# A planner that books a change of first partition, with one padded operand split in two, one product chain made a stream of its own and one fetch moved later

## The chip, the core and the metric

The kernel runs on one core of one Trainium2 chip. The metric is device time in microseconds (us) of one execution on that core. Five engines work side by side, each through a queue of its own in program order: TensorE (PE: matmuls; PEld: its weight loads), VectorE (DVE), ScalarE (ACT), GpSimd (POOL) and SyncE (SP), which here only issues DMAs.

## What is computed

One decoder layer over 272 prompt rows (16 of them meta tokens) and 8 x 4 sample rows, 304 columns in all. Cut to what matters:

```python
xn = rms_norm(x, norm_mix);  z = xn @ w_in               # 2048 x 7456
z_a, z_b = z[..., :RWKV_COLS], z[..., RWKV_COLS:]
# RWKV-7 group, 16 heads of 64
S = S * w_t + sa * b_t + v_t * k_t;  o_t = S @ r_t        # per token, sa = S @ a_t
o = group_norm(o) * ln_w + ln_b
bonus = jnp.sum(rh * kh * r_k, axis=-1, keepdims=True) * vh
o_a = (o + bonus) * g
# retention group, 4 heads of 256, chunked
o_b = retention(z_b)
h = x + concat(o_a, o_b) @ w_out
h = h + (silu(rms_norm(h) @ w_gate) * (rms_norm(h) @ w_up)) @ w_down
y = rms_norm(h)
```

The outputs are y, the last projected rows and the new states.

## The kernel before, in words

**Main job list.** All weights go through one sequence of jobs (`sequence`, `main`): 59 column tiles of the input projection, 2 x 16 tiles of the output projection, then the FFN. A job runs k-steps; a k-step is three f32r matmuls into a PSUM bank `acc` (xh by wh, xl by wh, xh by wl, the operands split into a high and a low part), 304, 290 or 288 columns wide. Weights come by SP into `wr` (3 tiles of 1024 columns); ACT casts 512 columns at a time into `wh`, DVE forms the rest `wl`.

**Streams.** Everything else is a set of generators (`streams`), each of which issues a step and yields. Two heads together are a pair (`pair`, 8 of them). A pair prepares its operands, forms 64-token chunk scores against a zero-padded operand (`arp`, two heads side by side), inverts a triangular matrix (`inverse`: four small matmul groups, inv0 to inv3), computes the bonus (`bonus`), runs the state loop (`units`: for u = 0 to 4 three products, here called A, B and C of unit u), and normalises the output (`pair_out`). `by_token`, `sample` (the 8 x 4 sample rows, with their old state `s0`, 256 KB by DMA) and `ret` (the 4 retention heads) are streams too. Their matmuls are plain f32 into banks `mm`. In the state loop and in `inverse` the results go out of PSUM by halves: one instruction on partitions 0 to 63, one on 64 to 127 (`HALF`).

**What sets the order.** The program is built twice. In the draft, `Plan.book` prices each instruction and keeps a clock for each engine; `pick` lets a stream take its next step when its last step's results are ready by the plan's PE clock, and otherwise the main job goes on by one k-step. The picks are logged and the second build repeats them, so each engine's order is fixed when the kernel runs. Half-partition instructions are priced by `part`: DVE adds 80 ns, ACT adds 10 ns or takes 90 ns off when there is a per-partition scale. `Room` then gives each scratch tile a place in one arena by the draft's times (`place`, `pack`).

**The fetch of s0.** `lora_weights(p, 0)`, started when the pair's first input tile is out, issues the pair's low-rank weights and `s0` one behind the other on SP; `pair` waits for both.

Of the kernel before, what the change touches and what calls it, by code (L numbers as in the profile page):

```python
# [9 lines left out]
F32R = mybir.dt.float32r  # L10
# [5 lines left out]
P = 128  # L16
# [3 lines left out]
META = 16  # L20
NB = 8
# [57 lines left out]
WIDE = 4200  # L79
FREE, GAPS = 800.0, (2000.0, 1000.0, 500.0, 200.0, 0.0)  # L80

# [225 lines left out]
class Plan:  # L307
# [5 lines left out]
    def __init__(self, nc, rooms, draft, log, keep):  # L313
        self.keep = keep
        self.rooms, self.draft, self.log, self.count = rooms, draft, log, 0
        self.clock = dict(PE=0.0, DVE=0.0, ACT=0.0, POOL=0.0, SP=0.0)
        self.end = self.dma = 0.0
        self.uses, self.outside, self.banks = {}, (), set()
        self.mode, self.parts, self.empty, self.begun, self.idle = None, {}, 0.0, 0.0, 0.0
        self.taken = {"DVE": [], "POOL": []}  # L320
        self.streams, self.made = [], 0
# [27 lines left out]
    def book(self, eng, what, a, k):  # L349
# [20 lines left out]
        else:  # L370
            part = out.shape[0] < P
            each = sum(math.prod(x.shape[1:]) == 1 for x in ins) if n > 1 else 0
# [7 lines left out]
            else:  # L380
                dur, tail = (60 + 0.85 * n, 60) if what == "memset" else (125 + 0.8 * n, 65) if what == "tensor_copy" else (185 + 1.65 * n, 60)
            if part and eng == "DVE":
                dur += 80
            if part and eng == "ACT" and (each or n == 320):
                dur += 10 if ins[0].name not in self.banks else -90
            self.started = max(self.clock[eng], at)
            at = self.share(eng, what, ins, self.started, dur, each) + dur
# [36 lines left out]
    def array(self, what, out, w, x, ready):  # L424
# [15 lines left out]
        at = max(self.parts.get(part, self.empty), self.begun + 5)  # L440
        self.idle += max(0.0, ready - at)
        at = max(at, ready)
        self.begun = at
# [41 lines left out]
class Room:  # L485
# [20 lines left out]
    def place(self, limit):  # L506


        best = None
        for key in (lambda n, a, b, *_: (-n, a), lambda n, a, b, *_: (-n * (b - a), a), lambda n, a, *_: (a, -n),  # L510
                    lambda n, a, b, *_: (a - b, -n), lambda n, a, b, *_: (-n // 256, a - b)):
            for gap in GAPS:
                found = self.pack(key, limit, gap)
                if found is not None and (best is None or found[0] < best[0]):
                    best = found
        self.lack, self.size, self.places = best

    def pack(self, key, limit, gap):
        done, places, lack, end = [], [0] * len(self.spans), 0.0, 0
        used = [i for i, span in enumerate(self.spans) if span[1] is not None]  # L520
        for i in sorted(used, key=lambda i: key(*self.spans[i])):
            size, a, b, at, until = self.spans[i]
            size = -(-size // 8) * 8
            near = []
            for o, n, c, d, s, u in done:
                if a <= d and c <= b:
                    near.append((o, o + n, -1.0))
                else:
                    free = max(0.0, at - u if d < a else s - until)
                    if free < gap:  # L530
                        near.append((o, o + n, free))
            near.sort()
            best = None
            for o in sorted({0, *(e for _, e, _ in near)}):
                if o + size > limit:
                    break
                free = min((f for s, e, f in near if s < o + size and o < e), default=gap)
                if free > -1.0 and (best is None or free > best[0]):
# [3 lines left out]
            if best is None:  # L542
                return None
            lack += max(0.0, FREE - best[0])
# [21 lines left out]
class Step:  # L566
# [340 lines left out]
    def lora_weights(self, p, half, z):  # L907
# [3 lines left out]
        self.sp.dma_start(lw, self.I["lora"][p, :, 2 * half:2 * half + 2])  # L911
        if not half:
            z["s0"] = self.t([P, NB, 64], "s0")
            self.sp.dma_start(z["s0"], self.I["s0w"][p])
        yield
# [27 lines left out]
    def pair(self, p, z):  # L943
        cst, act, dve, pe, pool = self.cv, self.act, self.dve, self.pe, self.pool
        blk = cst("blk", P)
        while p >= PAIRS and ("mid", p - PAIRS) not in self.done:
            yield
        while not all(("lora", i) in self.done for i in range(3)) or len(z) < 5:
            yield
# [5 lines left out]
        pw = self.ps()  # L955
        k, r, v, s0, (wh, wl) = z["k"], z["r"], z["v"], z["s0"], z["lora", 0]
        xw, xa = self.xw
# [40 lines left out]
        dve.tensor_mul(bk[:, 1, :], kf, ee)  # L998
        dve.tensor_mul(ra[:, 1, META:], r[:, META:], dd[:, META:])
        yield  # L1000
        dve.tensor_mul(ta, ta, kk)
        dve.tensor_mul(ra[:, 0, :], kk, dp)
        arp = self.t([P, NU, 2, 2, 64], "arp")
        bku = self.t([P, NU, P], "bku")
# [4 lines left out]
        d4 = self.t([P, NB, 1], "d4")  # L1009
        pool.memset(arp[:, 0], 0.0)  # L1010
        for hi, h in enumerate(HALF):
            pool.memset(arp[h, 1:, :, 1 - hi], 0.0)
        pool.memset(bku[:, 0], 0.0)
        pool.memset(v0, 0.0)
        yield
        dve.tensor_mul(bk[:, 0, :], ta, ee)
        pool.memset(ax, 0.0)
        pool.memset(axd, 0.0)
# [9 lines left out]
        for hi, h in enumerate(HALF):  # L1028
            act.copy(arp[h, 0, 0, hi, :META], ra[h, 0, :META])
            act.copy(arp[h, 1:, :, hi], units(ra[h]))  # L1030

# [43 lines left out]
        for i, h in enumerate(HALF):  # L1075
            act.copy(sc[h, :, 0, i, :], arp[h, :, 0, i, :])
            pool.memset(sv[h, 0, i, :], 0.0)
# [13 lines left out]

    def bonus(self, r, kf, v, rkb):

# [6 lines left out]
        yield  # L1100
        bon = self.t([P, TO], "bon")
        self.dve.tensor_mul(bon[:, :SEQ], pq[:, :SEQ], v[:, META:NP])
        self.dve.tensor_mul(four(bon[:, SEQ:]), four(pq[:, SEQ:TO]), smp(v))
        return bon

# [106 lines left out]

    def units(self, p, sc, bkt, sv, sav, tt, arp, dl, o):

# [35 lines left out]
        for u in range(1, NU):  # L1250
            out = pt[:, (u - 1) * P:u * P]
            pe.matmul(out, flat(sv, u), arp[:, u, 1].rearrange("p h c -> p (h c)"), start=True, stop=False)
            pe.matmul(out, flat(sav, u), sc[:, u, 1].rearrange("p h c -> p (h c)"), start=False, stop=True)
# [516 lines left out]
def flat(a, u):  # L1770
    return a[:, u].rearrange("p h c -> p (h c)")
# [39 lines left out]
```

## Time and profile before

| | |
|---|---|
| median of 3 runs | 1567.49 us (1567.10 to 1567.64) |
| the profiled execution | 1568.03 us |
| its span, first to last instruction | 1566.0 us |
| instructions | 30584 |
| PE busy, PEld busy | 1545.0 us, 1509.6 us |
| DVE, ACT, POOL busy | 1097.1, 861.7, 27.9 us |
| granted TensorE clock, mean | 0.997 |

PE is the engine that hardly rests. A busy PE is not a PE at its peak: matmuls overlap and their ends are modelled. So a matmul's cost is read here from start to start in the timeline: what a matmul delays is the start of the next one. The mixing, with its streams, lies between about 60 and 640 us; after it only the main job list runs.

### The profile page before, as it was taken

To read this page: it belongs to the slowest core of one execution; us is meant where nothing else is said; L and a number is where in the kernel's file an instruction comes from. 1 tells how busy PE (TensorE), PEld (TensorE's weight loads), DVE (VectorE), ACT (ScalarE), POOL (GpSimd) and SP (SyncE) were. 2 spreads that over 40 slices of the span, in tenths; PEclk is the share of its full clock that TensorE was granted. 3 is DMA by queue.
4 is the path that set the end of the run, shared out by engine and by line. 5 is a ranking of instruction groups with operands and counts; after the bars stand their busy time and mean duration, and the time that the engine had idled before them with its cause. 6 is when DMAs were issued, how large, how long until landed. Compare 5 with 4: busy or idle time off the path is not lost.

```text
span 1566.0 us, 30584 instructions
## 1 busy us (share of the span) xinstructions
PE 1545.0 (99%) x11388; PEld 1509.6 (96%) x11388; DVE 1097.1 (70%) x2783; ACT 861.7 (55%) x2008; POOL 27.9 (2%) x145
## 2 busy tenths in 40 slices
PE   9999999999999999999999999999999999999997
PEld 8999999998989999999999999999999999999997
DVE  7899888987989776776555565555565656565657
ACT  6777878687777655555444444444444444444445
POOL 1000000000000000000000000000000000000000
PEclk9999999999999999999999999999999999999998
DMA  7543433434544536755555555555555555555553
GB/s 256 158 145 113 119 113 124 133 97 137 193 148 147 196 121 238 247 164 161 163 173 162 169 159 171 162 164 168 168 161 175 161 164 163 173 164 169 157 173 118
DMA packets 76995, 252.46 MB, mean 161 GB/s; under 512 B 9392, under 2 KB 14640, under 8 KB 76848
## 3 DMA queue, kind: packets, MB, share of 16 engines
q1 hardware_dynamic: 76848, 250.52, 51.0%
q8 instruction: 90, 1.47, 0.4%
q14 instruction: 57, 0.47, 0.1%
HBM read 236.21 MB, written 14.28 MB: 160 GB/s over the span
## 4 chain that ended last, share of the span: by engine, by line
PE 72%; DVE 3%; ACT 3%; issue 1%; DVEq 0%; ACTq 0%
PE acc L302 67%; PE mm L302 6%; DVE arena_dt.float L302 2%; ACT arena_dt.float L302 2%; DVE wl L302 1%; ACT wh L302 0%; ACT arena_dt.float32r L302 0%; DVE arena_dt.float32r L302 0%; DVEq L1807 0%; ACT shout L302 0%; ACTq L302 0%; DVEq L302 0%
## 5 line engine op out<-in xcount | busy, mean ns | idle before, releaser
L302 PE MATMUL acc<-xh,wh 128*128 128x288 f32 (+2 forms) x2592 | 795.6, 307 | 0.0
L302 PE MATMUL acc<-xh,wl 128*128 128x288 f32 (+2 forms) x2592 | 769.2, 297 | 0.0
L302 PE MATMUL acc<-xl,wh 128*128 128x288 f32 (+2 forms) x2592 | 767.4, 296 | 0.0
L302 ACT CAST wh<-wr 128x512 fp32r<-128x512 f32 x826 | 501.2, 617 | 347.5 <-PE acc L302 331.2
L302 DVE TENSOR_TENSOR wl<-wr,wh 128x512 fp32r<-128x512 f32 x826 | 561.3, 687 | 133.7 <-ACT wh L302 131.1
L302 PEld LDWEIGHTS acc<-xl,wh 128*128 128x128 f32 x2592 | 489.7, 189 | 4.2 <-issue 1.0
L302 PEld LDWEIGHTS acc<-xh,wh 128*128 128x128 f32 x2592 | 488.4, 188 | 4.7 <-issue 1.8
L302 PEld LDWEIGHTS acc<-xh,wl 128*128 128x128 f32 x2592 | 486.1, 188 | 0.4
L302 PE MATMUL acc<-arena_dt.float32r,wh 128*128 128x288 f32 x1408 | 282.4, 296 | 0.4 <-ACT arena_dt.float32r L302 0.3
L302 PEld LDWEIGHTS acc<-arena_dt.float32r,wh 128*128 128x128 f32 x1408 | 226.0, 188 | 0.8 <-ACT arena_dt.float32r L302 0.5
L302 PE MATMUL acc<-arena_dt.float32r,wl 128*128 128x288 f32 x704 | 208.0, 295 | 0.0
L302 DVE TENSOR_TENSOR arena_dt.float<-acc,arena_dt.float 128x288 f32<-128x288 f32 (+4 forms) x181 | 72.8, 421 | 166.9 <-PE acc L302 166.4
L302 DVE TENSOR_TENSOR arena_dt.float<-arena_dt.float 128x288 f32<-128x288 f32 (+23 forms) x697 | 179.7, 288 | 12.0 <-ACT arena_dt.float L302 5.2
L302 PE MATMUL mm<-arena_dt.float 128*128 128x128 f32 (+5 forms) x1072 | 170.3, 312 | 4.0 <-ACT arena_dt.float L302 2.6
L302 ACT ACTIVATE arena_dt.float<-arena_dt.float 128x288 f32<-128x288 f32 (+6 forms) x242 | 103.9, 436 | 118.9 <-DVE arena_dt.float L302 117.2
L302 DVE TENSOR_TENSOR arena_dt.float<-arena_dt.float,acc 128x288 f32<-128x288 f32 x208 | 94.4, 454 | 105.9 <-PE acc L302 105.6
L302 PEld LDWEIGHTS mm<-arena_dt.float 128*128 128x128 f32 (+1 forms) x1072 | 137.4, 181 | 21.9 <-ACT arena_dt.float L302 8.6
L302 PEld LDWEIGHTS acc<-arena_dt.float32r,wl 128*128 128x128 f32 x704 | 132.0, 187 | 0.0
L302 ACT COPY arena_dt.float<-mm 64x64 f32<-64x64 f32 (+11 forms) x330 | 91.9, 287 | 68.7 <-PE mm L302 62.1
L302 ACT CAST arena_dt.float32r<-arena_dt.float 128x288 fp32r<-128x288 f32 (+4 forms) x73 | 30.4, 422 | 89.6 <-DVE arena_dt.float L302 89.4
L302 ACT COPY arena_dt.float<-arena_dt.float 128x32 f32<-128x32 f32 (+9 forms) x219 | 55.5, 301 | 10.8 <-DVE arena_dt.float L302 9.7
L302 DVE SCALAR_TENSOR_TENSOR arena_dt.float<-arena_dt.float 128x288 f32<-128x288 f32 (+3 forms) x100 | 43.8, 441 | 3.3 <-ACT arena_dt.float L302 1.5
(63 smaller groups left out, 565.7 us busy)
## 6 DMA issues: line engine op xcount, KB each, us to landing
wr<-big SPq DMA_DIRECT2D x409, 512.0 KB, 3.6
arena_dt.float<-s0r SPq DMA_DIRECT2D x16, 512.0 KB, 6.6
out_rts<-arena_dt.float SPq DMA_DIRECT2D x16, 512.0 KB, 5.9
arena_dt.float<-xT SPq DMA_DIRECT2D x4, 576.0 KB, 6.0
out_y<-arena_dt.float SPq DMA_DIRECT2D x8, 288.0 KB, 2.4
arena_dt.float<-xT SPq DMA_DIRECT2D x7, 304.0 KB, 6.0
wr<-big SPq DMA_DIRECT2D x8, 256.0 KB, 5.8
arena_dt.float<-lora SPq DMA_DIRECT2D x16, 128.0 KB, 3.6
```

The costliest lines, as they stand in the source:

```text
L302: return self._plan.keep(f(*a, **k))
```

## The change

- `Plan.book`: the `part` prices go. Instead the plan keeps, for DVE and ACT, the first partitions of the last instruction's output and first input. Where the next instruction's differ, the engine's clock moves on by the instruction's tail (83 to 94 ns) plus 31 ns (DVE) or 25 ns (ACT) before it starts. `array` adds 90 ns to an f32 matmul that the plan sees waiting over 20 ns.
- `Room.place` and `pack`: other sort keys; a tile that finds no place is moved to the front and the packing tried again; the widest spare time that gives any packing is kept.
- `arp` becomes `au` (all chunks) and `ru` (without chunk 0): the score product, one matmul of 256 columns for each of chunks 1 to 4, becomes two of 128; two more ACT copies and two more POOL memsets for each pair.
- `bonus` leaves the pair's chain and is added as a stream as soon as its inputs stand.
- `s0` is fetched by `pair`, behind the last operand products, instead of by `lora_weights`.

The diff, cut to its core:

```diff
-            part = out.shape[0] < P
...
-            if part and eng == "DVE":
-                dur += 80
-            if part and eng == "ACT" and (each or n == 320):
-                dur += 10 if ins[0].name not in self.banks else -90
-            self.started = max(self.clock[eng], at)
+            key = (out.start_partition(), ins[0].start_partition() if ins else 0)
+            ready = self.clock[eng]
+            if eng != "POOL" and key != self.part[eng]:
+                ready += tail + (25 if eng == "ACT" else 31)
+                self.part[eng] = key
+            self.started = max(ready, at)
...
+        if ready > at + 20 and w.dtype != F32R:
+            dur += 90
...
-                if found is not None and (best is None or found[0] < best[0]):
+                order = sorted((i for i, span in enumerate(self.spans) if span[1] is not None), key=lambda i: key(*self.spans[i]))
+                for _ in range(TRIES):
+                    found = self.pack(order, limit, gap)
...
+                    order.remove(found)
+                    order.insert(0, found)
...
-        if not half:
-            z["s0"] = self.t([P, NB, 64], "s0")
-            self.sp.dma_start(z["s0"], self.I["s0w"][p])
...
+        bon = self.t([P, TO], "bon")
+        self.plan.add(self.bonus(bon, r, kf, v, rkb), 1 + p)
...
-        arp = self.t([P, NU, 2, 2, 64], "arp")
+        au = self.t([P, NU, 2, 64], "au")
+        ru = self.t([P, NU - 1, 2, 64], "ru")
...
         dve.tensor_mul(bk[:, 0, :], ta, ee)
+        s0 = self.t([P, NB, 64], "s0")
+        self.sp.dma_start(s0, self.I["s0w"][p])
...
-            act.copy(arp[h, 1:, :, hi], units(ra[h]))
+            act.copy(au[h, 1:, hi], ra[h, 0, META:NP].rearrange("p (u c) -> p u c", c=64))
+            act.copy(ru[h, :, hi], ra[h, 1, META:NP].rearrange("p (u c) -> p u c", c=64))
...
-                pe.matmul(pt[:, j * 2 * P:(j * 2 + n) * P], bku[:, u],
-                          arp[:, u, :n].rearrange("p q h c -> p (q h c)"), start=True, stop=True)
+                for q in range(n):
+                    c = (j * 2 + q) * P
+                    pe.matmul(pt[:, c:c + P], bku[:, u], flat(ru, u - 1) if q else flat(au, u), start=True, stop=True)
...
-        bon = yield from self.bonus(r, kf, v, rkb)
-        yield
-        yield from self.units(p, sc, bkt, sv, sav, tt, arp, dl, o)
+        yield from self.units(p, sc, bkt, sv, sav, tt, ru, dl, o)
```

The first place where the order moves is PE in the state loop of the first pair, between product C of unit 0 (the first `mm`) and product A of unit 1 (the last `mm`). Before:

```order
L302 MATMUL mm_1934<-arena_dt.float_70 128x128
L302 MATMUL acc_1908<-xh_72,wh_1787 128x304
L302 MATMUL acc_1908<-xl_73,wh_1787 128x304
L302 MATMUL acc_1908<-xh_72,wl_1788 128x304
L302 MATMUL acc_1908<-xh_72,wh_1825 128x304
L302 MATMUL acc_1908<-xl_73,wh_1825 128x304
L302 MATMUL acc_1908<-xh_72,wl_1826 128x304
L302 MATMUL mm_1950<-arena_dt.float_70 128x128
```

Now, where the three `acc` rows ahead of the last `mm` stand a second time that is not repeated here:

```order
L302 MATMUL mm_1968<-arena_dt.float_70 128x128
L302 MATMUL acc_1890<-xl_73,wh_1829 128x304
L302 MATMUL acc_1890<-xh_72,wl_1830 128x304
L302 MATMUL acc_1890<-xh_72,wh_1858 128x304
L302 MATMUL acc_1890<-xl_73,wh_1858 128x304
L302 MATMUL acc_1890<-xh_72,wl_1859 128x304
L302 MATMUL mm_1994<-arena_dt.float_70 128x128
```

Two k-steps, six main matmuls, lay between the two products; now it is three k-steps.

The second place is SP's queue, around the first pair's low-rank weights (`lora`) and old state (`s0w`), between weight tiles (`wr`). Before:

```order
L302 DMA wr_447<-big 128x1024
L302 DMA arena_dt.float_70<-lora 128x256
L302 DMA arena_dt.float_70<-s0w 128x512
L302 DMA wr_512<-big 128x1024
L302 DMA wr_558<-big 128x1024
```

Now:

```order
L302 DMA wr_447<-big 128x1024
L302 DMA arena_dt.float_70<-lora 128x256
L302 DMA wr_511<-big 128x1024
L302 DMA wr_557<-big 128x1024
L302 DMA wr_606<-big 128x1024
L302 DMA wr_647<-big 128x1024
L302 DMA wr_696<-big 128x1024
L302 DMA wr_747<-big 128x1024
L302 DMA arena_dt.float_70<-lora 128x256
L302 DMA wr_795<-big 128x1024
L302 DMA wr_838<-big 128x1024
L302 DMA arena_dt.float_70<-s0w 128x512
```

The fetch moves behind eight weight tiles and the next pair's low-rank weights.

The third place is DVE where the output projection begins: `xl` x8 makes the low parts of the first eight mixed tiles, and the 128x288 product with an `mm` bank is the last step of the last pair. Before:

```order
L302 TENSOR_TENSOR arena_dt.float_70<-arena_dt.float_70,mm_7694 128x288
L302 TENSOR_TENSOR arena_dt.float_70<-acc_7653,arena_dt.float_70 128x304
L302 TENSOR_TENSOR wl_7746<-wr_7702,wh_7745 128x512
L302 TENSOR_TENSOR wl_7763<-wr_7702,wh_7762 128x512
L302 TENSOR_TENSOR wl_7781<-wr_7743,wh_7780 128x512
L302 TENSOR_TENSOR wl_7797<-wr_7743,wh_7796 128x512
L302 TENSOR_TENSOR xl_73<-arena_dt.float_70,xh_72 128x288 x8
```

Now:

```order
L302 TENSOR_TENSOR arena_dt.float_70<-arena_dt.float_70,mm_7767 128x288
L302 TENSOR_SCALAR arena_dt.float32r<-arena_dt.float32r,cst_266 128x256
L302 TENSOR_TENSOR wl_7807<-wr_7657,wh_7806 128x512
L302 SCALAR_TENSOR_TENSOR arena_dt.float_70<-arena_dt.float_70,mm_7822 128x512
L302 SCALAR_TENSOR_TENSOR arena_dt.float_70<-arena_dt.float_70,mm_7823 128x512
L302 TENSOR_SCALAR arena_dt.float32r<-arena_dt.float32r,cst_266 128x256
L302 TENSOR_TENSOR xl_73<-arena_dt.float_70,xh_72 128x288 x8
```

A whole input tile lay between the last pair's end and `xl`; now the state update of a retention head (the two `mm` updates of 128x512 and a scaling) stands there instead.

## Rows read from the trace of the kernel before

**Rows 1.** The page: busy time, share of the span, instructions of each engine

```profile
PE 1545.0 (99%) x11388; PEld 1509.6 (96%) x11388; DVE 1097.1 (70%) x2783; ACT 861.7 (55%) x2008; POOL 27.9 (2%) x145
```

**Rows 2.** Windows: length, busy us (instructions) by engine, clock, DMA share, GB/s

```profile
60.00:640.00 580.00, 572.40 (x4109) 541.00 (x4108) 492.95 (x1662) 411.53 (x1178) 22.47 (x111) 1.00 0.46 148
720.00:1520.00 800.00, 800.00 (x6027) 800.00 (x6026) 467.82 (x836) 338.70 (x592) 0.00 (x0) 1.00 0.54 166
```

**Rows 3.** Waits of PE's weight loads: us in total, times, longest

```profile
PEld mm L302 <- ACT arena_dt.float L302: 12.0, 33, 0.9
...
PEld mm L302 <- DVE arena_dt.float L302: 0.7, 3, 0.2
```

**Rows 4.** Timeline of PE, the first pair's state loop: start us, us, what

```profile
143.68 0.30 PE L302 MATMUL acc<-xh,wl 128*128 128x304 f32 x1
144.36 0.49 PE L302 MATMUL mm<-arena_dt.float 128*128 128x128 f32 x2 [0.38 <-ACT arena_dt.float L302]
...
144.82 0.31 PE L302 MATMUL acc<-xl,wh 128*128 128x304 f32 x1
...
147.52 0.30 PE L302 MATMUL acc<-xh,wl 128*128 128x304 f32 x1
147.65 0.38 PE L302 MATMUL mm<-arena_dt.float 128*128 128x128 f32 x2
...
148.02 0.30 PE L302 MATMUL acc<-xl,wh 128*128 128x304 f32 x1
```

**Rows 5.** Timeline of PE, first and last of the late f32 matmuls

```profile
31.13 0.77 PE L302 MATMUL mm<-arena_dt.float,ones 128*128 128x304 f32 x2
...
569.80 1.24 PE L302 MATMUL mm<-arena_dt.float,ones 128*128 128x288 f32 x4
```

**Rows 6.** Timeline of ACT, the same state loop: half-partition instructions

```profile
141.12 0.65 ACT L302 ACTIVATE arena_dt.float<-mm,arena_dt.float 64x64 f32<-64x64 f32 x2 [0.73 <-PE mm L302]
...
142.31 1.53 ACT L302 ACTIVATE arena_dt.float<-arena_dt.float 64x64 f32<-64x64 f32 x4
143.87 0.44 ACT L302 COPY arena_dt.float<-mm 64x64 f32<-64x64 f32 x2
```

**Rows 7.** Timeline of ACT, eight scalings in a row on all partitions

```profile
120.37 2.02 ACT L302 ACTIVATE arena_dt.float<-arena_dt.float,cst 128x64 f32<-128x64 f32 x8
```

**Rows 8.** Timeline of DVE, the state update by halves in the same loop

```profile
146.41 0.59 DVE L302 SCALAR_TENSOR_TENSOR arena_dt.float<-mm,arena_dt.float 64x64 f32<-64x64 f32 x2
```

**Rows 9.** Timeline of PE, two 256-column f32 matmuls, then four 128-column ones

```profile
73.29 1.02 PE L302 MATMUL mm<-arena_dt.float 128*128 128x256 f32 x4
...
74.28 0.30 PE L302 MATMUL acc<-xl,wh 128*128 128x288 f32 x1
...
125.04 1.05 PE L302 MATMUL mm<-arena_dt.float 128*128 128x128 f32 x8
...
126.06 0.29 PE L302 MATMUL acc<-xl,wh 128*128 128x288 f32 x1
```

**Rows 10.** Issue to landing: eight fetches of s0w, then sixteen of s0r

```profile
DMA to landing us min/median/max: 3.5/3.9/5.3
...
DMA to landing us min/median/max: 3.5/6.6/8.6
```

**Rows 11.** Timeline of SP: the third retention head's four fetches of s0r

```profile
535.19 1.81 SPq L302 DMA_DIRECT2D arena_dt.float<-s0r  x4
```

**Rows 12.** DVE groups by shape: count, busy us, mean ns, idle before

```profile
L302 DVE SCALAR_TENSOR_TENSOR arena_dt.float<-arena_dt.float,mm 128x512 f32<-128x512 f32 x32 | 20.5, 684 | 0.6 <-PE mm L302 0.5
```

**Rows 13.** Timeline of PE: the first two matmuls of the output projection

```profile
592.52 0.30 PE L302 MATMUL acc<-xh,wh 128*128 128x288 f32 x1
592.81 0.40 PE L302 MATMUL acc<-xl,wh 128*128 128x288 f32 x1
```

More of the change, by code (lines that the diff above doesn't have):

```diff
@@ L79 @@
 WIDE = 4200
-FREE, GAPS = 800.0, (2000.0, 1000.0, 500.0, 200.0, 0.0)
+FREE, GAPS, TRIES = 800.0, (2000.0, 1000.0, 500.0, 200.0, 50.0, 0.0), 12
 def zcols():
@@ L320, in __init__ @@
         self.taken = {"DVE": [], "POOL": []}
+        self.part = {"DVE": (0, 0), "ACT": (0, 0)}
         self.streams, self.made = [], 0
@@ L509, in place, with pack @@
         best = None
[L510 to L513, printed above, removed]
-                if found is not None and (best is None or found[0] < best[0]):
-                    best = found
+        for gap in GAPS:
+            for key in (lambda n, a, b, *_: (-n, a), lambda n, a, b, *_: (-n * (b - a), a), lambda n, a, b, *_: (a - b, -n),
+                        lambda n, a, b, *_: (-n // 256, a - b), lambda n, a, b, *_: (-n // 512, a)):
+                order = sorted((i for i, span in enumerate(self.spans) if span[1] is not None), key=lambda i: key(*self.spans[i]))
+                for _ in range(TRIES):
+                    found = self.pack(order, limit, gap)
+                    if not isinstance(found, int):
+                        if best is None or found[0] < best[0]:
+                            best = found
+                        break
+                    order.remove(found)
+                    order.insert(0, found)
+            if best is not None:
+                break
         self.lack, self.size, self.places = best
-    def pack(self, key, limit, gap):
+    def pack(self, order, limit, gap):
         done, places, lack, end = [], [0] * len(self.spans), 0.0, 0
-        used = [i for i, span in enumerate(self.spans) if span[1] is not None]
-        for i in sorted(used, key=lambda i: key(*self.spans[i])):
+        for i in order:
             size, a, b, at, until = self.spans[i]
@@ L529, in pack @@
                     free = max(0.0, at - u if d < a else s - until)
-                    if free < gap:
+                    if free < 2000.0:
                         near.append((o, o + n, free))
@@ L536, in pack @@
                     break
-                free = min((f for s, e, f in near if s < o + size and o < e), default=gap)
+                free = min((f for s, e, f in near if s < o + size and o < e), default=2000.0)
                 if free > -1.0 and (best is None or free > best[0]):
@@ L542, in pack @@
             if best is None:
-                return None
+                return i
             lack += max(0.0, FREE - best[0])
@@ L947, in pair @@
             yield
-        while not all(("lora", i) in self.done for i in range(3)) or len(z) < 5:
+        while not all(("lora", i) in self.done for i in range(3)) or len(z) < 4:
             yield
@@ L955, in pair @@
         pw = self.ps()
-        k, r, v, s0, (wh, wl) = z["k"], z["r"], z["v"], z["s0"], z["lora", 0]
+        k, r, v, (wh, wl) = z["k"], z["r"], z["v"], z["lora", 0]
         xw, xa = self.xw
@@ L1009, in pair @@
         d4 = self.t([P, NB, 1], "d4")
-        pool.memset(arp[:, 0], 0.0)
+        pool.memset(au[:, 0], 0.0)
         for hi, h in enumerate(HALF):
-            pool.memset(arp[h, 1:, :, 1 - hi], 0.0)
+            pool.memset(au[h, 1:, 1 - hi], 0.0)
+            pool.memset(ru[h, :, 1 - hi], 0.0)
         pool.memset(bku[:, 0], 0.0)
@@ L1028, in pair @@
         for hi, h in enumerate(HALF):
-            act.copy(arp[h, 0, 0, hi, :META], ra[h, 0, :META])
-            act.copy(arp[h, 1:, :, hi], units(ra[h]))
+            act.copy(au[h, 0, hi, :META], ra[h, 0, :META])
+            act.copy(au[h, 1:, hi], ra[h, 0, META:NP].rearrange("p (u c) -> p u c", c=64))
+            act.copy(ru[h, :, hi], ra[h, 1, META:NP].rearrange("p (u c) -> p u c", c=64))
         act.copy(ax[:, :, 0:4], smp(ra[:, 0, :]))
@@ L1075, in pair @@
         for i, h in enumerate(HALF):
-            act.copy(sc[h, :, 0, i, :], arp[h, :, 0, i, :])
+            act.copy(sc[h, :, 0, i, :], au[h, :, i, :])
             pool.memset(sv[h, 0, i, :], 0.0)
@@ L1090, in pair, with bonus @@
         self.done.add(("pair", p))
-    def bonus(self, r, kf, v, rkb):
+    def bonus(self, bon, r, kf, v, rkb):
         rkc = self.t([P, TO], "rkc")
@@ L1100, in bonus @@
         yield
-        bon = self.t([P, TO], "bon")
         self.dve.tensor_mul(bon[:, :SEQ], pq[:, :SEQ], v[:, META:NP])
         self.dve.tensor_mul(four(bon[:, SEQ:]), four(pq[:, SEQ:TO]), smp(v))
-        return bon
     def by_token(self, p, v, v0, bku, bkt, sv, sav):
@@ L1211, in inverse, with units @@
         return tt
-    def units(self, p, sc, bkt, sv, sav, tt, arp, dl, o):
+    def units(self, p, sc, bkt, sv, sav, tt, ru, dl, o):
         act, dve, pe, pool = self.act, self.dve, self.pe, self.pool
@@ L1251, in units @@
             out = pt[:, (u - 1) * P:u * P]
-            pe.matmul(out, flat(sv, u), arp[:, u, 1].rearrange("p h c -> p (h c)"), start=True, stop=False)
+            pe.matmul(out, flat(sv, u), flat(ru, u - 1), start=True, stop=False)
             pe.matmul(out, flat(sav, u), sc[:, u, 1].rearrange("p h c -> p (h c)"), start=False, stop=True)
```

## The prediction

> **What bounds the kernel now.** The page's first part comes first: PE is busy 99% of the span [rows 1]. The windows then show two regimes [rows 2]. After the mixing PE does 6027 matmuls in 800 us, one each 0.133 us, with nothing in between; the change touches nothing there. In the mixing, 60 to 640 us, PE is also nearly always busy, but between the main job's matmuls stand f32 matmuls of the streams, and these can come late. The granted clock is full, 1.00 (2.4 GHz), in both windows, so no clock effect is to be won or lost in them.
>
> Whether an f32 matmul comes late is read from start to start. Without a wait, the step from the main matmul ahead of it to the second main matmul behind it is 0.50 us (147.52 to 148.02), two main matmuls of 0.14 and one f32 product of 0.22, so changing between the two kinds costs 0.01 at most [rows 4]. With a wait the same step is 1.14 us (143.68 to 144.82), 0.64 late, and the row names ACT [rows 4]. I did this for all 225 places at which f32 matmuls interrupt the main job: 70 are late by more than 0.05 us, the first by 0.12, the last by 0.19 [rows 5], and the sum is 22.4 us. By stream: state loop 37 places, 12.1 us; sample rows 7, 2.7; inverse 7, 2.6; bonus 4, 1.1; output norms 6, 1.3; the pair's first norm 3, 0.8; retention 3, 0.7; the rest 1.1. The waits of the weight loads say who is late: ACT 12.0 us in 33 waits, DVE 0.7 in 3 [rows 3]. So 22.4 us is the most that a better order can win; PE's own work stays.
>
> **Part 1, the booked change of first partition.** The plan sends a stream's next matmul when it believes the step before to be done. So a late matmul is a step that was booked too short. The state loop's halves show by how much. Four ACT scalings that go from one half of the partitions to the other take 1.53 us, 0.38 each [rows 6]; eight on all partitions take 2.02, 0.25 each [rows 7], though they move as many columns. The old plan books 108 + 0.83 x 64 + 90 + 10 = 0.26 us, the new one 0.25 + 0.094 + 0.025 = 0.37. Two copies from PSUM take 0.44 [rows 6]: old 0.24, new 0.48. Unit 0's two scalings from PSUM take 0.65 [rows 6]: old 0.24, new 0.66. DVE's two updates take 0.59 [rows 8]: old 0.55, new 0.62. So the new prices are within 0.05 us of the rows everywhere, and the old plan was short, for each pair, by 0.41 (unit 0's scalings) + 5 x 0.20 (copies) + 4 x 0.24 (scalings) + 4 x 0.04 (updates) = 2.5 us, 20 us over 8 pairs. Of that 12.1 came out as lateness, since matmuls are only placed every k-step (0.42 us) and the rounding up hides the rest.
>
> The order shows that the steps do move. Product A of unit 1 has 0.83 us of PE work ahead of it in four of eight pairs before, and 1.05 to 1.9 in seven of eight now (5.9 in the other); product B of unit 1 has 0.83 to 2.5 before, 1.66 to 5.0 now; product B of unit 0 had at most 0.83 in six pairs before, and has at least 1.12 in all now. More room costs nothing: the main job fills it. I keep a quarter of the state loop's lateness, 3.0 us, for queues that the plan still misjudges: gain 9.1, between 0 (every step is late again in its new place) and 12.1. Inverse: carrying each late step's need over to its new room leaves 0.9 of 2.6, gain 1.7 (0 to 2.6).
>
> **Part 2, the bonus as a stream.** Its matmul had 2.4 to 7.4 us of room and was still late, 1.1 us in all; now the product is formed much earlier and nothing behind it in the pair's chain waits. Gain 0.9 (0 to 1.1).
>
> **Part 3, two score operands.** Two 256-column matmuls and the two main ones behind take 0.99 us (73.29 to 74.28), four of 128 columns 1.02 (125.04 to 126.06) [rows 9]. 16 such groups: loss 0.03 x 16 = 0.5. There are 233 interruptions instead of 227; at 0.01 each that is nothing. The additional copies (ACT, 2 for each pair) and memsets (POOL) cost about 16 x 0.2 us on engines that are busy 71% and 4% of the mixing window [rows 2]; if that cover fails, the steps behind are late by that 0.2 us, 3.2 us in all at most.
>
> **Part 4, the late fetch.** From the place of the fetch to the sample rows' first matmul the order now has 12 to 20 us of PE work; landing took 3.5 to 5.3 us [rows 10]. Hidden, cost 0. Behind it on SP stand weight tiles; a fetch that waited for its place in the arena would hold them, but in all eight pairs the place's last user stands at least 10 us of PE work earlier, so I expect none.
>
> **Part 5, what the new order moves elsewhere.** Output projection: DVE forms `xl` now behind the state update of a retention head. From its matmuls PE has six main matmuls to do (0.84) and the first of the projection (0.13); DVE has two updates of 0.684 [rows 12], a scaling and the first `xl`, about 0.8 together, 2.2 in all: 1.2 us late, against 0.15 + 0.10 before, where the first two starts lie 0.29 apart instead of 0.13 [rows 13]. Loss 0.9 (0 to 2). Retention: the states `s0r` of one head land 3.5 to 8.6 us after issue [rows 10], and the work between issue and first use shrinks from 4.6 to 9.7 us to 4.4 to 7.9. SP runs ahead of the plan, 12 to 14 us before the use in the rows (535.19 against a first use at 549.72) [rows 11], so I take 0.5 (0 to 7). The sample rows, the other norms and the rest, 6.6 us with the retention, have causes that the change doesn't price; I take 0.4 off (-3 to +3).
>
> **The sum.** -9.1 - 1.7 - 0.9 + 0.5 + 0.9 + 0.5 - 0.4 = -10.2 us. The profiled execution's own time is 1568.03, so 1557.8 in a profile. It lies 0.54 above the median of the three runs; in median terms 1557.3.
>
> **Rivals.** (a) *The longer halves on ACT are no matter of partitions.* If 0.38 against 0.25 came from something else (the kind of operand, say), the new ACT prices would only shift steps and the late ones would be late again. Only DVE's 0.04 us and the bonus would be mended: 8 x 4 x 0.04 + 0.9 = 2.2 us won, against 0.5 + 0.9 + 0.5 = 1.9 lost: 1567. Against it, copies and scalings are both longer by the same 0.1 us in halves [rows 6, 7]. With it goes any other way in which the room is used up again. 0.13. The Trainium skill, page "VectorE: DVE Perf Modes", section "Two Vector instructions with no wait between them", says that a Vector instruction which starts in another quadrant of partitions than the last one is held until all earlier ones are done; it says this of Vector alone. Taken as complete it would make this rival right for ACT; rows 6 and 7 differ from it.
>
> (b) *Retention states land late.* Place: the matmuls of a query with the old states, four heads. Arena places are now freed at the very program point of the fetch in two heads, so SP can't run ahead there. With 4.4 us of room in three heads and 5.0 in one, and a landing of 8.6 [rows 10], PE waits 3 x 4.2 + 3.6 = 16.2 us: 1557.3 - 0.5 + 16.2 = 1573. It turns the sign from 10.2 us of such waits on. Against it: in the rows the third head's fetches are 14 us ahead of the use [rows 11], and a landing of 6.6 is the middle. 0.06.
>
> (c) *The room heals more than the loop.* ACT's copies in halves also stand ahead of sample steps and norms in the same queue; if all but 5 us of the 22.4 goes, 1568.03 - 17.4 + 1.9 - 0.54 = 1552. 0.15.
>
> **Chances.** Forecast 0.66, (c) 0.15, (a) 0.13, (b) 0.06. About 0.2%, 3.1 us, is what a measurement can tell from no change. Faster is the forecast and (c), less a tenth of the forecast's cases that end too small: 0.76; same 0.18; slower 0.06. The range takes in (c) at its lower end and, above, half of the loop's gain lost together with 3 us of late states: 1557.3 + 4.6 + 3 = 1565.
>
> **What would show it.** Right: fewer waits of weight loads on ACT, 4 to 6 us instead of 12.0; state-loop steps of 0.50 us from main matmul to main matmul behind unit 0 and at product B of unit 1; the same 0.133 us for each FFN matmul. Part 5 shows in a gap of over 1 us at the first `xl` matmul of the projection. Wrong: half-partition scalings of 0.25 us, late state loops in spite of 1.2 us of room, or long waits in the retention's 32-column matmuls.

## The result and the profile after

The changed kernel takes 1556.65 us (median of 4 runs, 1555.96 to 1558.81) against 1567.57 of the kernel before in the same series (4 runs, 1567.10 to 1568.38): ratio 0.9932, 95% interval 0.9915 to 0.9949. The forecast was 1557.3. The profiled execution took 1555.96 us, its span 1554.1 against 1566.0 before, 11.9 less.

The first part of the page and the two windows, to be held against [rows 1] and [rows 2]:

```profile
PE 1536.7 (99%) x11452; PEld 1510.3 (97%) x11452; DVE 1098.1 (71%) x2783; ACT 863.5 (56%) x2024; POOL 28.2 (2%) x161
```

```profile
60.00:640.00 580.00, 576.35 (x4257) 553.36 (x4256) 498.52 (x1669) 416.85 (x1201) 22.84 (x123) 1.00 0.49 155
710.00:1510.00 800.00, 800.00 (x6027) 800.00 (x6027) 467.47 (x835) 337.30 (x590) 0.00 (x0) 1.00 0.55 166
```

DVE's and ACT's work is what it was, and behind the mixing there are still 6027 matmuls in 800 us at a granted clock of 1.00 (2.4 GHz). So the gain lies in the mixing. The waits of PE's weight loads, us in total, times and longest, against [rows 3]:

```profile
PEld mm L302 <- issue: 3.7, 12, 1.1
PEld mm L302 <- DMA arena_dt.float<-s0r: 3.7, 4, 1.2
...
PEld acc L302 <- DVE xl L302: 1.5, 1, 1.5
...
PEld mm L302 <- ACT arena_dt.float L302: 1.2, 3, 0.6
...
PEld mm L302 <- DVE arena_dt.float L302: 1.0, 4, 0.4
```

The waits on ACT are down from 12.0 us in 33 to 1.2 in 3. One new row of 3.7 us names the retention's old states `s0r`, and the row of the operand `xl` has grown from 0.2 to 1.5. In the first pair's state loop, PE's timeline reads (start us, us, what), against [rows 4]:

```profile
146.19 0.30 PE L302 MATMUL acc<-xh,wl 128*128 128x304 f32 x1
146.33 0.38 PE L302 MATMUL mm<-arena_dt.float 128*128 128x128 f32 x2
146.47 0.39 PE L302 MATMUL acc<-xh,wh 128*128 128x304 f32 x1
146.70 0.30 PE L302 MATMUL acc<-xl,wh 128*128 128x304 f32 x1
```

From 146.19 to 146.70 are 0.51 us: the step without a wait. Measured from start to start as in the prediction, 35 of 231 places are late by more than 0.05 us, 12.2 us in all, against 70 of 225 and 22.4 before.

### The profile page after: what moved, and what is told of

It is laid out like the page before. It is cut to its first block, busy times and chain, and to the rows that moved or that the text cites. A ratio compares the mean times of both kernels' runs of the same rounds, so it can differ in the third digit from the quotient of the medians.

```text
span 1554.1 us, 30759 instructions
## 1 busy us (share of the span) xinstructions
PE 1536.7 (99%) x11452; PEld 1510.3 (97%) x11452; DVE 1098.1 (71%) x2783; ACT 863.5 (56%) x2024; POOL 28.2 (2%) x161
## 4 chain that ended last, share of the span: by engine, by line
PE 87%; DVE 6%; issue 4%; ACT 2%; DMA 1%; POOL 0%; SPq 0%; DVEq 0%; ACTq 0%; POOLq 0%
PE acc L302 78%; PE mm L302 9%; DVE arena_dt.float L302 4%; DVE wl L302 2%; ACT arena_dt.float L302 2%; DMA arena_dt.float<-s0r 1%; ACT wh L302 0%; DMA arena_dt.float<-xT 0%; POOL arena_dt.float L302 0%; SPq L302 0%; ACT arena_dt.float32r L302 0%; DVE arena_dt.float32r L302 0%; DVEq L1818 0%; ACT xh L302 0%; DVE xl L302 0%
## 5 line engine op out<-in xcount | busy, mean ns | idle before, releaser
L302 DVE TENSOR_TENSOR arena_dt.float<-arena_dt.float 128x288 f32<-128x288 f32 (+25 forms) x697 | 181.0, 287 | 12.1 <-ACT arena_dt.float L302 4.4
L302 PE MATMUL mm<-arena_dt.float 128*128 128x128 f32 (+8 forms) x1136 | 169.1, 301 | 1.9 <-DMA arena_dt.float<-s0r 1.8
L302 PEld LDWEIGHTS mm<-arena_dt.float 128*128 128x128 f32 (+1 forms) x1136 | 142.7, 181 | 14.9 <-DMA arena_dt.float<-s0r 3.7
L302 ACT COPY arena_dt.float<-mm 64x64 f32<-64x64 f32 (+10 forms) x330 | 92.3, 287 | 57.2 <-PE mm L302 52.9
```

Source lines behind the costliest of these rows:

```text
L302: return self._plan.keep(f(*a, **k))
```

## The experiments

The theory was that the gain comes from booking the change of first partition, on ScalarE above all; the rivals, that it comes from the other edits or that ScalarE's halves are long for another reason. Later runs follow what came up: the arena. In the table, "late" is the sum in the profiled execution over all f32 places, of it the places that begin with a pair's step (state loop, inverse, scores, norms) and with a retention head's. Each ratio is to the kernel before in the same series, whose medians were 1567.09 to 1567.57 us.

| kernel | median us | ratio to before, 95% | late us (places) | pair | retention |
|---|---|---|---|---|---|
| before | 1567.57 | | 22.4 (70) | 18.0 | 0.7 |
| changed | 1556.65 | 0.9915 to 0.9949 | 12.2 (35) | 4.9 | 4.8 |
| old_prices | 1574.76 | 1.0033 to 1.0067 | 29.8 (72) | 18.8 | 4.9 |
| dve_prices_only | 1570.09 | 1.0010 to 1.0029 | 26.0 (79) | 17.7 | 3.1 |
| act_prices_only | 1558.16 | 0.9934 to 0.9963 | 13.2 (33) | 6.0 | 5.4 |
| old_packing | 1560.48 | 0.9946 to 0.9975 | 17.5 (36) | 6.7 | 8.6 |
| early_fetch | 1564.15 | 0.9969 to 0.9988 | 22.1 (31) | 9.8 | 10.1 |
| booking_on_before | 1613.89 | 1.0276 to 1.0310 | 56.4 (53) | 37.6 | 9.1 |
| margin | 1579.98 | 1.0063 to 1.0091 | 35.1 (25) | 23.6 | 5.9 |
| state_price | 1556.07 | 0.9910 to 0.9939 | 13.0 (36) | 5.0 | 6.1 |
| state_price_8 | 1561.57 | 0.9948 to 0.9973 | 19.2 (44) | 14.3 | 1.9 |
| state_price_12 | 1558.68 | 0.9929 to 0.9959 | 13.8 (40) | 9.0 | 0.0 |
| state_places | 1555.77 | 0.9910 to 0.9938 | 11.4 (37) | 5.5 | 3.6 |

The late sum accounts for most of the time: old_prices is 17.6 us later than the changed kernel and 18.1 longer, margin 22.9 and 23.3. It does so least for booking_on_before, 44.2 and 57.2, and early_fetch, 9.9 and 7.5.

**Which prices make the gain.** Three kernels with the change's other edits and other prices. The old prices:

```diff
...
-            if eng != "POOL" and key != self.part[eng]:
-                ready += tail + (25 if eng == "ACT" else 31)
-                self.part[eng] = key
...
+            if part and eng == "DVE":
+                dur += 80
+            if part and eng == "ACT" and (each or n == 320):
+                dur += 10 if ins[0].name not in self.banks else -90
...
```

> The changed kernel with the old prices for half-partition instructions; the split operand, the bonus stream, the late fetch and the new packing stay. Theory (the gain is the booked change of first partition): the state loop's products come late again, some 10 to 12 us of weight-load waits on ACT, 1564 to 1569 us. Rival (the gain comes from the other edits, which give the streams more room in the arena): about 1557 as the changed kernel, with under 3 us of waits on ACT.

The new price on VectorE alone:

```diff
...
-            if eng != "POOL" and key != self.part[eng]:
-                ready += tail + (25 if eng == "ACT" else 31)
+            if part and eng == "ACT" and (each or n == 320):
+                dur += 10 if ins[0].name not in self.banks else -90
+            if eng == "DVE" and key != self.part[eng]:
+                ready += tail + 31
```

> The changed kernel with the new price for VectorE alone; ScalarE's halves are booked as before. Theory (ScalarE's prices were the short ones, by 0.1 to 0.2 us for each half, VectorE's by 0.04): nearly nothing of the gain is kept, 1563 to 1568 us, weight-load waits on ACT of 9 to 12 us. Rival (VectorE's short prices let every later step of the loop slip): 1557 to 1560.

The new price on ScalarE alone:

```diff
-            if eng != "POOL" and key != self.part[eng]:
-                ready += tail + (25 if eng == "ACT" else 31)
+            if eng == "DVE" and out.shape[0] < P:
+                dur += 90
+            if eng == "ACT" and key != self.part[eng]:
+                ready += tail + 25
```

> The changed kernel with the new price for ScalarE alone; VectorE's halves keep a fixed price, 90 ns in place of 80 (0.57 us for the two updates that took 0.59). Theory: the whole gain stays, 1555 to 1559 us, weight-load waits on ACT of 1 to 3 us. Rival (both engines are needed): 1561 to 1565, with waits on DVE of over 4 us.

The first row of the weight loads' waits on ACT, of these three in this order:

```profile
PEld mm L302 <- ACT arena_dt.float L302: 16.4, 34, 1.5
```

```profile
PEld mm L302 <- ACT arena_dt.float L302: 12.1, 29, 1.2
```

```profile
PEld mm L302 <- ACT arena_dt.float L302: 0.4, 2, 0.2
```

The theory holds: with ScalarE's old price the waits stand at 16.4 and 12.1 us, with the new one at 0.4; VectorE's price matters little (1558.16 against 1556.65). In the later kernels that are the changed one with another thing altered and the same ScalarE price, this row lies between 1.0 and 7.4 us, so the two groups stay apart, but by less than these three rows show. The two highest are early_fetch and state_price_8:

```profile
PEld mm L302 <- ACT arena_dt.float L302: 7.4, 10, 2.5
```

```profile
PEld mm L302 <- ACT arena_dt.float L302: 7.4, 11, 2.5
```

Both old-price kernels came out longer than expected, and longer than the kernel before (by 7.7 and 3.0 us of the same series): without ScalarE's price the other edits win nothing. Whether they lose time by themselves is not shown, since plans that differ in one price of the retention alone lie up to 5.5 us apart (1556.07 and 1561.57). The 90 ns that `array` adds for a matmul that waits is among these other edits and was not tried alone.

**Is it the change of partitions?** A tail of small instructions behind the last output, 64 partitions by 64 columns each, without a per-partition scale (`f` gives a series' output half and input; `one` scales by 2).

```diff
...
+            for t, f in enumerate(tests):
+                one(gap[:, t:t + 1], src[:, :1])
+                for i in range(8):
+                    h, x = f(i)
+                    one(dst[h, i, :], x)
```

> The changed kernel with a tail behind its last output: on ScalarE, then on VectorE, eight series of eight instructions on 64 partitions x 64 columns, a small instruction on all partitions ahead of each. From SBUF: (1) all on the lower half, (2) halves in turn, (3) only the output in turn, (4) only the input in turn. From PSUM: (5) all lower, (6) halves in turn. Input in turn from SBUF and PSUM: (7) lower half of SBUF and upper of PSUM, (8) lower of both. Theory (an instruction waits for its forerunner's end where the first partition of output or input changes): on both engines (1), (5) and (8) short, ScalarE 0.16 to 0.27 us each, (2), (3), (4), (6) longer by about 0.1, and (7) longer too, as the planner books it. Rival (ScalarE's longer halves come from the kind of operand): (1) as long as (2) and (5) as (6) on ScalarE. The Trainium skill, page "VectorE: DVE Perf Modes", section "Two Vector instructions with no wait between them", keeps the last start for SBUF and PSUM apart; by it (7) would be as short as (8) on VectorE.

ScalarE's timeline, series (1) to (6), of the first seven instructions, of the others eight:

```profile
1548.28 1.11 ACT L302 ACTIVATE arena_dt.float<-arena_dt.float 64x64 f32<-64x64 f32 x7
1549.54 2.19 ACT L302 ACTIVATE arena_dt.float<-arena_dt.float 64x64 f32<-64x64 f32 x8
1551.87 2.20 ACT L302 ACTIVATE arena_dt.float<-arena_dt.float 64x64 f32<-64x64 f32 x8
1554.19 2.20 ACT L302 ACTIVATE arena_dt.float<-arena_dt.float 64x64 f32<-64x64 f32 x8
1556.52 0.96 ACT L302 ACTIVATE arena_dt.float<-mm 64x64 f32<-64x64 f32 x8
...
1557.44 1.93 ACT L302 ACTIVATE arena_dt.float<-mm 64x64 f32<-64x64 f32 x8
```

On one half the starts lie 0.146 us apart (SBUF) and 0.103 (PSUM); with halves in turn 0.28 and 0.24, and a change of the output's or the input's start alone costs as much. So the hold is 0.135 us on ScalarE, where the plan books 0.119; [rows 6] and [rows 7], 0.38 against 0.25, differ by the same 0.13. VectorE, series (1) and (2):

```profile
1560.88 1.08 DVE L302 TENSOR_SCALAR arena_dt.float<-arena_dt.float 64x64 f32<-64x64 f32 x7 [10.87 <-ACT arena_dt.float L302]
1562.05 1.72 DVE L302 TENSOR_SCALAR arena_dt.float<-arena_dt.float 64x64 f32<-64x64 f32 x8
```

Its starts lie 0.13 apart on one half (mean from the second step on) and 0.22 in turn, a hold of 0.09, where the plan books 0.114 for an operation like this one. Rival (a) of the prediction is out. Series (7), the input in turn from the lower half of SBUF and the upper of PSUM, ScalarE:

```profile
1559.64 0.20 ACT L302 ACTIVATE arena_dt.float<-mm 64x64 f32<-64x64 f32 x1
1559.74 0.24 ACT L302 ACTIVATE arena_dt.float<-arena_dt.float 64x64 f32<-64x64 f32 x1
1559.89 0.21 ACT L302 ACTIVATE arena_dt.float<-mm 64x64 f32<-64x64 f32 x1
```

Two starts take 0.25 us, the same as in series (8), where both inputs are lower (1560.87 to 1561.14 and on to 1561.38). So nothing is held there, and the plan, which keeps one start for both memories, books too much in that case. The first step of series (8) shows the reverse:

```profile
1560.59 0.25 ACT L302 ACTIVATE arena_dt.float<-arena_dt.float 64x64 f32<-64x64 f32 x1
1560.87 0.22 ACT L302 ACTIVATE arena_dt.float<-mm 64x64 f32<-64x64 f32 x1
```

Both inputs are lower, yet the step takes 0.28 us (0.22 on VectorE): the last input from PSUM, in series (7), was the upper half. The Trainium skill, page "VectorE: DVE Perf Modes", section "Two Vector instructions with no wait between them", keeps the two apart. VectorE agrees (0.24 for two), and ScalarE, of which the section says nothing, behaves alike.

**What the other edits are for.** Booking on the kernel before, with the change's search for places; the old search finds no arrangement at all.

```diff
-FREE, GAPS = 800.0, (2000.0, 1000.0, 500.0, 200.0, 0.0)
+FREE, GAPS, TRIES = 800.0, (2000.0, 1000.0, 500.0, 200.0, 50.0, 0.0), 150
...
-            if part and eng == "DVE":
-                dur += 80
...
+            if eng != "POOL" and key != self.part[eng]:
+                ready += tail + (25 if eng == "ACT" else 31)
...
```

> The kernel before with the booked change of first partition and the new search for arena places (150 tries; only the search with no spare time between two users of a place finds any); the operand in one tile, the bonus in the chain, the fetch early. Theory (booking makes the gain; the other edits make room for it): the waits on ACT fall from 12.0 to under 4 us, 1556 to 1562 us, with some new waits for places. Rival (the gain needs the other edits for itself): 1565 to 1569.

Both expectations missed: it is 46.6 us longer than before, and 34.0 of it are lateness at f32 places. Longer booked steps make the scratch tiles live longer: in the plan's own lists the tiles alive at once reach 28360 of 28952 columns, against 26160 in the kernel before, and places could only be found with no spare time between one user and the next. The changed kernel has 27232 alive at once, and its search ends at 2 us. At 210.10 PE waits 3.37 us; behind it stand, on POOL and ACT:

```profile
209.29 0.21 POOL L302 MEMSET arena_dt.float<- 128x128 f32 x1 [31.84 <-DVE arena_dt.float L302]
```

```profile
209.54 0.42 ACT L302 COPY arena_dt.float<-mm 64x64 f32<-64x64 f32 x2 [1.41 <-POOL arena_dt.float L302]
```

A memset needs no data: what DVE ends there is the last use of the place, and the copies for PE stand behind the memset. So the split operand, the late fetch and the bonus as a stream pay for the longer lives: with them, the same prices find places with spare time. With the bonus put back into the chain, the changed kernel would have 29808 columns alive at once, more than there are. What the split operand gives by itself was not separated.

Long waits of PE can cost more than their own length, for the granted clock falls with them. In the trace of booking_on_before PE starts nothing between 206.43 and 210.10 us. The window behind that, and two main matmuls in it:

```profile
210.00:213.00 3.00, 2.90 (x12) 2.93 (x13) 2.48 (x8) 1.32 (x4) 0.00 (x0) 0.50 0.58 153
```

```profile
211.43 0.46 PE L302 MATMUL acc<-xh,wh 128*128 128x304 f32 x1
211.68 0.46 PE L302 MATMUL acc<-xl,wh 128*128 128x304 f32 x1
```

At a granted clock of 0.50 (1.2 GHz) the main matmuls start 0.25 us apart, against 0.14 at 1.00. In the first 700 us of this trace 30.6 us run so, so at most 15 of its 46.6 us lie there (an estimate: half the time), in part counted in the lateness. It is 17.0 us in margin, 3.4 each in early_fetch, old_packing and state_price_8, and none in the other traces, before and changed included.

The early fetch, with 150 tries at 1 us of spare time:

```diff
...
         self.sp.dma_start(lw, self.I["lora"][p, :, 2 * half:2 * half + 2])
+        if not half:
+            z["s0"] = self.t([P, NB, 64], "s0")
+            self.sp.dma_start(z["s0"], self.I["s0w"][p])
...
-        s0 = self.t([P, NB, 64], "s0")
-        self.sp.dma_start(s0, self.I["s0w"][p])
+        s0 = z["s0"]
```

> The changed kernel with the samples' old state fetched where it was before, with the low-rank weights; since the state then lives longer, the search for places needs more tries (150 for 12). Theory (the late fetch is hidden, it is there for the arena): 1555.5 to 1558.5 us. Rival (the late fetch delays weight tiles or the sample rows): 1552 to 1555.

Both missed: 1564.15, from 1560.72 (mean granted clock 0.997) to 1567.28 (0.994). The retention's states are 10.1 us late in all, and there is one more memset that waits, most likely for a place:

```profile
406.30 2.16 POOL L302 MEMSET arena_dt.float<- 128x128 f32 x11 [10.40 <-ACT arena_dt.float L302]
```

So the late fetch is likely worth something by the room it leaves. How much of the 7.5 us is due to that, and how much to the plan having been drawn anew, stays open (see the state prices below). The old search for places (`place` and `pack` as before), with the changed kernel's order of instructions:

```diff
...
-                order = sorted((i for i, span in enumerate(self.spans) if span[1] is not None), key=lambda i: key(*self.spans[i]))
-                for _ in range(TRIES):
-                    found = self.pack(order, limit, gap)
...
+            for gap in GAPS:
+                found = self.pack(key, limit, gap)
...
```

> The changed kernel with the old search for arena places. The order of the instructions on each engine stays, only the places of scratch tiles move. Theory (the order makes the gain, the places do not): 1555 to 1559 us. Rival (spare time between two users of a place makes part of it): 1560 or more, with waits that name tiles of other streams.

3.8 us longer than the changed kernel, of which the retention's states make the most (8.6 us late against 4.8). The second theory, that places don't matter, fell: every engine's order is the changed kernel's.

**More room for each step.**

```diff
-                ready += tail + (25 if eng == "ACT" else 31)
+                ready += tail + (125 if eng == "ACT" else 131)
```

> The changed kernel with each change of first partition booked 0.1 us dearer on both engines. Theory (the prices fit, the state loop keeps only 1.8 us of lateness): the loop wins 1 us at most; the room of the states is 3.9 and 4.8 us in two heads, so 2 to 3 us of waits stay there, 1555 to 1558 us. Rival (the loop's steps are still booked too short): 1552 to 1554.

Both fell, and the rival was half right. Up to 400 us only 4 places are late, 1.1 us in all, where the changed kernel has 24 and 6.3. But the pairs end later, and the main job runs out of tiles that need no pair's output. The PE groups from 551.7 to 605.5 hold no `acc` matmul; the first two of the five:

```profile
L302 PE MATMUL mm<-arena_dt.float 128*128 128x128 f32 (+5 forms) x226 | 33.4, 337 | 6.6 <-ACT arena_dt.float L302 4.3 <-DVE arena_dt.float L302 1.6 <-DMA arena_dt.float<-s0r 0.7
L302 PE MATMUL mm<-arena_dt.float32r 128*128 128x512 f32 (+2 forms) x18 | 6.1, 444 | 2.5 <-DVE arena_dt.float32r L302 1.6 <-ACT arena_dt.float32r L302 1.0
```

For 54 us the streams have nothing to hide behind, and two of this trace's stretches at the lower clock lie here and just behind (three windows of 20 us from 560 to 620 have 0.92, 0.91 and 0.91).

**The waits for the retention's states.** In the changed kernel, SP and PE at head 0:

```profile
383.74 1.75 SPq L302 DMA_DIRECT2D arena_dt.float<-s0r  x4
```

```profile
388.89 1.68 PE L302 MATMUL mm<-arena_dt.float 128*32 128x256 f32 x20
391.25 0.63 PE L302 MATMUL mm<-arena_dt.float 128*32 128x256 f32 x7 [0.67 <-DMA arena_dt.float<-s0r]
```

The fetch starts 5 us ahead of the use, where [rows 11] had 14. The first answer was a price: the plan lets these states land later, by 3600 in the first run, 8000 and 12000 in the next two (the expectations say 8.6 and 12.6 us; it was 8.0 and 12.0).

```diff
-            done = self.dma + 600
+            done = self.dma + (3600 if out.name.startswith("s0r") else 600)
```

> The changed kernel with one more price: the plan lets the retention's old states land 3.6 us after their transfer in place of 0.6, so their matmuls are sent later. Theory (the two heads that wait 1.8 and 2.3 us for these states are pure loss): the waits go, 1551.5 to 1554 us. Rival (the head's time is set by the fetch's late start, and what follows in the head waits in its place): 1556 to 1558.

> The price for the landing of the retention's old states raised further, from 3.6 to 8.6 us behind the transfer. In the plan's own times, the room from the moment a state's place in the arena is left by its last user to the state's first use was 5.6 us in head 0 and 3.4 in head 1 of the changed kernel, where the waits were 1.8 and 2.3, and 8.1 or more in the others, where there were none; with the price of 3.6 it was still 5.9 and 2.5; now it is at least 8.4 everywhere. Theory (the waits come from places that are left too late): no wait of a 32-row matmul on the states above 0.5 us, 1551.5 to 1553.5 us. Rival (the transfers themselves are slow in that stretch, or the waits move to the next step): 1555 to 1558.

> The same price raised by 4 us more, 12.6 us behind the transfer; the room is 7.3 us for one state and 17 or more for the others. Theory: nothing is left to win at the states, 1551.5 to 1554 us; the heads end later, which the main job covers. Rival (each microsecond that a head is held lengthens the mixing): 1556 or more.

The price of 3.6 us hardly binds, since the plan had 12 to 16 us between issue and use: nothing won. The higher ones end the waits (at most 0.6 us and none), but the pairs' steps are 9.4 and 4.1 us later than in the changed kernel, so neither gains. At 340.40 of state_price_8, 3.26 us late by a wait of 2.25 and by matmuls at the lower clock behind it, a copy that PE needs stands on ACT behind one that waits for DVE. The same copy in the changed kernel comes second:

```profile
339.57 0.21 ACT L302 COPY arena_dt.float<-arena_dt.float 128x8 f32<-128x8 f32 x1 [2.51 <-DVE arena_dt.float L302]
```

```profile
336.41 0.20 ACT L302 COPY arena_dt.float<-arena_dt.float 128x8 f32<-128x8 f32 x1
```

Up to 384 us of the changed kernel every engine's order is the same in these two traces, since the price first counts at head 0. So this wait comes with the arena: a new price draws the order anew from there on, but all places, also the earlier ones. Among the kernels with the changed kernel's ScalarE price that differ from it in one other thing, itself included, the pair's lateness came out anywhere from 4.9 to 14.3 us. (The three kernels with ScalarE's old price lie above that, at 17.7 to 18.8; so do booking_on_before and margin.) That is why the last run keeps the order and moves places only:

```diff
...
+        elif x.name.startswith("s0r") and i not in self.states:
+            self.states.add(i)
+            span[3] = at - 8000
...
+            if best is None or i in self.states and best[0] < 0:
                 return i
...
```

> The changed kernel with the order of every engine's instructions kept, only the places in the arena searched anew so that a retention state's place is left at least 8 us ahead of the state's first use, where there is such a place. In the plan's times the least room of head 0 grows from 5.6 to 9.2 us; head 1 keeps 3.4, there is no other place. Theory (the wait at the states is the transfer's time less this room): the 1.8 us of head 0 go, the 2.3 of head 1 stay, 1554.3 to 1555.5 us. Rival (the waits have another cause): 1556 to 1557.

```profile
380.16 1.84 SPq L302 DMA_DIRECT2D arena_dt.float<-s0r  x4
```

```profile
389.55 1.93 PE L302 MATMUL mm<-arena_dt.float 128*32 128x256 f32 x32
```

Head 0's fetch starts 3.6 us earlier and its wait goes from 1.82 to 0.34 us; head 1's stays, 2.44 against 2.25. The mechanism is shown by these waits, not by the time: at 1555.77 us (1554.91 to 1556.31), between the theory's range and the rival's, the kernel is 0.9 below the changed one, which is less than can be told apart, so it doesn't count as a better version.

## Why the prediction was right, step by step

| term | forecast us | measured us |
|---|---|---|
| state loop | -9.1 | 12.1 to 1.8: -10.3 |
| inverse | -1.7 | 2.6 to 2.1: -0.5 |
| bonus | -0.9 | 1.1 to 0.9: -0.3 |
| score operands | +0.5 | not separated |
| first `xl` of the output projection | +0.9 | 0.25 to 1.38: +1.1 |
| retention | +0.5 | 0.7 to 4.8: +4.1 |
| sample rows, norms, the rest | -0.4 | -3.1 |
| not foreseen | 0 | -2.3 |
| sum (span) | -10.2 | -11.9, of which 0.6 fall on no term |

- **State loop.** The central step held in mechanism and size: the old price of ScalarE was short, and the other edits together do not heal the loop without it. Nor does the price without them (booking_on_before). The waits on ACT fell further than the 4 to 6 us that were named.
- **Rivals.** (a) is out by the measured halves. (c) came in part: norms and sample rows healed too, but 12.2 us of lateness stayed, not 5.
- **Inverse and bonus** were over-rated by 1.2 and 0.6 us. The bonus's place in the order moved, but its lateness hardly did; why was not tested.
- **The late fetch at 0** was right as far as the sample rows go (2.7 to 1.1 us late). That the operand, the bonus as a stream, the fetch and the search have their worth in the arena had no term in the prediction: they were costed as copies and waits only, and without the first three the booked prices lose 46.6 us.
- **"More room costs nothing: the main job fills it"** holds for this change and has an end close by: 0.1 us more for each change of partition exhausts it. That no clock effect is to be won or lost held for the change too, but not for kernels whose PE waits longer.
- **Two slips** change nothing: the step of 0.99 us in Part 3 holds two f32 matmuls and one main one, not two, on both sides of the comparison; and the chance of "faster" adds up to 0.74, not 0.76.
- **Output projection.** The gap of over 1 us came as described:

```profile
577.09 0.29 PE L302 MATMUL acc<-xh,wh 128*128 128x288 f32 x1
578.60 0.40 PE L302 MATMUL acc<-xl,wh 128*128 128x288 f32 x1 [1.22 <-DVE xl L302]
```

- **Retention** is the term that was mis-sized: 0.5 taken, 4.1 measured, inside the 0 to 7. Rival (b) was right about the place and the mechanism in two heads, 1.82 and 2.25 us, and too large in all. The reason given against it, that SP runs 12 to 14 us ahead, was read from a head whose fetch started early. In the changed kernel the last two heads still have 15 us, but the fetch of head 0 starts 5 us ahead of its use.
- **Not foreseen.** A wait of 1.56 us for `wh` at 468.02 of the kernel before is gone, and the start of the program is 0.7 shorter; both follow from the new order and were not examined. The retention's miss of 3.6 us was made good by these and by the sample rows and norms. So it is luck that the total came within 0.7 us: it is closer than its terms.

## What to carry to other kernels

Where a plan made ahead of time sets the order, a price that is short by 0.1 us for each instruction on the engine in between comes back as waits of the engine that bounds the kernel; look for the instruction whose duration depends on its forerunner. A longer booked step must be paid for in memory and in work to hide behind, so count the tiles alive at once and the work left over before giving steps more room. And try a cure with order and places held fixed as far as can be: a plan drawn anew can move more than the effect that is looked for.

## What the runs showed of the hardware

- ScalarE holds an instruction when the first partition of its output or of its input differs from the last one's (halves of 64 partitions): 0.28 us from start to start against 0.146 from SBUF, 0.24 against 0.103 from PSUM. VectorE: 0.22 against 0.13 from SBUF.
- The start is kept for SBUF and PSUM apart on both engines: inputs in turn from lower SBUF and upper PSUM stay at 0.125 (ScalarE) and 0.12 us (VectorE), and a step from lower SBUF to lower PSUM takes 0.28 and 0.22 where the last input from PSUM was the upper half.
- In booking_on_before TensorE's granted clock was 0.50 (1.2 GHz) from 210 to 213 us, behind 3.67 us without a matmul's start, and main matmuls of 304 columns started 0.25 us apart, against 0.14 at 1.00.
